# Four first-layer MLP products ahead of the last transposes, and first-layer staging moved to the other side of SBUF

## The chip, the cores and the metric

One Trainium2 chip, one of its cores. The metric is the device time of one execution in microseconds (us): the median of three runs of the kernel before is 3024.37 us (3020.51 to 3025.22). The engines are named as the profile names them: PE (TensorE; its weight loads are PEld), ACT (ScalarE), DVE (VectorE), POOL (GpSimd), and SP, the engine whose queue issues every DMA of this kernel, in order.

## The reference

One transformer layer on 2048 tokens of width 1024, all in float32. What matters here is its second half, after attention and pooling have been merged and projected:

```
x = layernorm(ALPHA * x + g1 * y, ln1_g, ln1_b)          # x1, the input of the MLP
u = layernorm(x) * (1 + scale) + shift                   # 2048 x 1024
h = square(relu(u @ w1)) @ w2                            # w1: 1024 x 4096, w2: 4096 x 1024
x = layernorm(ALPHA * x + g2 * h, ln2_g, ln2_b)
```

## The kernel before

**Numbers in two halves.** A float32 operand is split into a rounded high part (ACT casts it, line 59) and the rest (DVE subtracts, line 62). A product of two split operands is three matmuls: high by high, high by low, low by high.

**Seven products instead of eight.** Both MLP layers multiply 2 x 2 blocks with seven products (`ORDER = (1, 6, 2, 7, 5, 4, 3)`), which need sums of blocks. The sums of `u` ("combinations") are made by `u2_half` (line 922) and written to DRAM in `us_scr[c]`, one plane for each product. The sums of the weights `w1` are made in SBUF by `Pair.add` and `Pair.step` on POOL; the sums of `w2` by `w2_fill` (line 1173), which also stores two of them in DRAM (`t3_scr`, `t2_scr`) for later products.

**Stages.** The stage ahead of the MLP works on two token halves (`c` = 0, 1; 1024 tokens each). Its last loop projects (`out_mm`), then normalises one block of 128 tokens after another (`ln_affine` to x1, `ln1_u` to the normalised `xn`). `u2_half(h)` takes four blocks: for each of four pairs of channels `kp` it transposes on PE (line 929), scales on ACT into `u2f` (line 930), makes four sums on POOL into `u2s` (lines 935 to 938), and stores both (SP, lines 941 and 942). The second half of `c` = 0 waits in the list `late` and runs early in `c` = 1. The second half of `c` = 1 needs the last block, so `run(late)` stands at the end of the stage.

**First layer** (from `mp = ctx.enter_context(sbuf("mlp"))`). 32 pairs of weight column blocks: 16 on the first 1024 tokens, 16 on the second. `Pair.load` brings a pair's raw weights (`sraw`, 1 MB as two DMAs, line 1001), `step` splits one operand into a tile `R`, `prod` (line 1039) does 12 matmuls, and its sums and squares go into tiles of the tag `st`. `l_fill(c, p)` loads the combination of product `p` (`rw`, 1 MB, line 1085) and splits it into two tiles `La` or `Lb`. The list `seq` gives the order of the products: the first two pairs go together (p = 1 for both, p = 6 for both, and so on). Seven `R` steps and all seven `l_fill` stand ahead of the first product.

**Second layer.** For each `p`, eight products of 48 matmuls (`prod2`, line 1254). All eight use the eight weight tiles of `p` (`L2[p]`, from the same 11 `La` tiles); meanwhile `w2_fill` makes those of the next `p`, and `h_fill` loads and splits the stored first-layer results two products ahead. The first tiles of `p` = 1 are made during the last pair of the first layer (`w2_first`, line 1107; `h_first`).

**What sets the order.** PE's instructions follow the program from the first layer on (`manual_schedule`). Those of ACT, DVE, POOL and SP are ordered, when the kernel is built, by a planner that simulates times: an instruction can be put ahead of others that the program has earlier, as soon as its inputs and its tile are there. Tiles come from pools with a number of buffers for each tag. A pool whose space a closed pool held comes behind it in this order: the planner places the first instruction on its tiles after the last one on the closed pool's tiles. On the chip a new tile waits only for the old tiles at its own addresses. In the kernel before, the MLP's pools `mlp` and `mlp1` (left side of SBUF) come after all of `lp` (left), `ptp` and `rp` (right side) are closed, behind `run(late)`; `mlp2` comes after `mlp1` is closed (`m1.close()`).

Of the kernel before, what the change touches and what calls it, by code (L numbers as in the profile page):

```python
# [10 lines left out]
F32 = mybir.dt.float32  # L11
F32R = mybir.dt.float32r
# [4 lines left out]
P = 128  # L17
# [19 lines left out]
def block_kernel(  # L37
# [5 lines left out]
    pe, act, dve, pool, sp = nc.tensor, nc.scalar, nc.vector, nc.gpsimd, nc.sync  # L43
# [6 lines left out]
    us_scr = [tc.dram_tile([P, 7, 4, 512], F32, name=f"us_scr{c}") for c in range(2)]  # L50
    hs_scr = [[tc.dram_tile([P, 4, 16, P], F32, name=f"hs_scr{c}{p}") for p in range(7)] for c in range(2)]
    t2_scr, t3_scr = (tc.dram_tile([P, 16, 512], F32, name=n) for n in ("t2_scr", "t3_scr"))

    def sbuf(name, side="left"):
        return tc.tile_pool(name=name, bufs=1, side=side, reuse_waits="tile")

    def split(hi, lo, src, lo_eng=None, hi_eng=None):
        if hi_eng is None:
            act.copy(hi, src)  # L59
        else:  # L60
            hi_eng.tensor_copy(hi, src)
        (lo_eng or dve).tensor_tensor(lo, src, hi.bitcast(F32), ALU.subtract)  # L62
# [53 lines left out]
    def slot(where, i, shape, dt, name):  # L116
        pl, tag, n = where
        return pl.tile(shape, dt, name=name, tag=f"{tag}{i}", bufs=n)
# [214 lines left out]
    def run(units):  # L333
        for f in units:
            f()
# [277 lines left out]
    for n, (b, g) in enumerate(order):  # L613
# [4 lines left out]
        for tok in (PLAN[g] if b + 2 < NB else TPLAN).split():  # L618
            t, i = tok[0], int(tok[1:] or 0)
# [36 lines left out]
    lpx = ExitStack()  # L656
# [67 lines left out]
    late = []  # L724
    for c in range(2):
        t0 = c * CH
# [3 lines left out]
        xs, ys = ((rp, "a", 8), (lp, "b", 9)) if c == 0 else ((lp, "b", 9), (rp, "a", 8))  # L730
# [95 lines left out]
        for n in range(4):  # L826
            w = wcols(w_in, 2048 + n * 256)
            for jj in range(2):
                ps = [ps2("ps_ga") for _ in HALF]
                chan_mm(ps, w, jj * P, um)  # L830
                s = slot(ys, 0, [P, CH], F32, "sa")
# [8 lines left out]
        for kk in range(4):  # L840
            raw = raw_tile([P, 2, CH])
            sp.dma_start(raw, a_scr[:, 2 * kk:2 * kk + 2, t0:t0 + CH])
            for k in range(2):
                hv = []
                for h in range(2):
                    t = slot(xs, h, [P, 2, 512], F32R, "av")
# [4 lines left out]
        for n in range(4):  # L851
            w = wcols(w_ab, n * 256) if n else w_first
            for jj in range(2):
                j = 2 * n + jj
# [3 lines left out]
                for h, (a, m) in enumerate(HALF):  # L858
                    s = sa[j][:, a:a + m]
                    dve.tensor_tensor(s, ps[h], s, ALU.mult)  # L860
                    pool.tensor_tensor(s, s, m0[j][:, a:a + m], ALU.add)  # L861
                    t = slot(xs if c == 1 and j == 0 else ys, h, [P, 2, 512], F32R, "mg")
# [51 lines left out]
        xn = []  # L914
# [3 lines left out]
            normal(n, accs[b])  # L918
            xn.append(n)

        def u2_half(h, c=c, t0=t0, xn=xn, ys=ys):

            for kp in range(4):
                f = slot(ys, 0, [P, 2, 512], F32, "u2f")
                for kk in range(2):
                    k = 2 * kp + kk
                    ps = ps2("ps_u2", "u", 2)
                    for i in range(4):
                        pe.transpose(ps[:, i * P:(i + 1) * P], xn[4 * h + i][:, k * P:(k + 1) * P], ident)
                    act.activation(f[:, kk], ps, AF.Identity, scale=mod[:, 32 + k, 0:1], bias=mod[:, 24 + k, 0:1])  # L930
                v = f.rearrange("p k (b r t) -> p k b r t", r=2, t=P)
                a11, a12, a21, a22 = v[:, 0, :, 0], v[:, 1, :, 0], v[:, 0, :, 1], v[:, 1, :, 1]
                s = slot(ys, 1, [P, 4, 256], F32, "u2s")
                sv = [s[:, i].rearrange("p (b t) -> p b t", t=P) for i in range(4)]
                pool.tensor_tensor(sv[0], a21, a22, ALU.add)
                pool.tensor_tensor(sv[1], sv[0], a11, ALU.subtract)
                pool.tensor_tensor(sv[2], a11, a21, ALU.subtract)
                pool.tensor_tensor(sv[3], a12, sv[1], ALU.subtract)
                dst = us_scr[c][:, :, kp, h * 256:(h + 1) * 256]
                for pl, t in enumerate((a11, a12, a22)):  # L940
                    sp.dma_start(dst[:, pl].rearrange("p (b t) -> p b t", t=P), t)
                sp.dma_start(dst[:, 3:7], s)
# [5 lines left out]
        w2 = wcols(w_out, 512, gb[0][:, 512:768])  # L948
# [10 lines left out]
            if b == 5:  # L959
                u2_half(0)  # L960
        ln1_u(7)
        late = [lambda f=u2_half: f(1)]

    sp.dma_start(g2_scr, gb[1][0:1, :].rearrange("a d -> (a d)"))
    run(late)
    lpx.close()
    ptx.close()
    rpx.close()

# [5 lines left out]

    ORDER = (1, 6, 2, 7, 5, 4, 3)
    PLANE = {1: 0, 2: 1, 4: 2, 5: 3, 6: 4, 7: 5, 3: 6}
    mp = ctx.enter_context(sbuf("mlp"))
    m1 = ExitStack()
    m1p = m1.enter_context(sbuf("mlp1"))  # L980
    ms3 = ExitStack()
    ms3.enter_context(tc.manual_schedule(engines={mybir.EngineType.PE}))

    def rtile():
        return mp.tile([P, 2, 4, P], F32R, name="R", tag="R", bufs=8)

    def sttile(name):
        return m1p.tile([P, 512], F32, name=name, tag="st", bufs=14)

    w1v = w_mlp_in.rearrange("(k two p) n -> p two k n", two=2, p=P)  # L990

    class Pair:
# [3 lines left out]
            self.c, self.n, self.R = c, n, {}  # L996

        def load(self):
            self.raw = m1p.tile([P, 2, 4, 256], F32, name="sraw", tag="sraw", bufs=3)
            for k in range(2):  # L1000
                sp.dma_start(self.raw[:, k], w1v[:, k, :, self.n * 256:(self.n + 1) * 256])
            b11, b12, b21, b22 = self.b = [self.raw[:, k, :, h * P:(h + 1) * P] for k in range(2) for h in range(2)]
            self.op = {1: b11, 2: b21, 3: b22, 4: b11, 7: b12}

        def add(self):
            b11, b12, b21, b22 = self.b
            for p in (5, 6):
                self.op[p] = m1p.tile([P, 4, P], F32, name="ext", tag="ext", bufs=4)
            pool.tensor_tensor(self.op[5], b12, b11, ALU.subtract)
            pool.tensor_tensor(self.op[6], b22, self.op[5], ALU.subtract)  # L1010
            pool.tensor_tensor(b12, b22, b12, ALU.subtract)
# [69 lines left out]

    def l_fill(c, p):

        raw = m1p.tile([P, 4, 512], F32, name="rw", tag="rw", bufs=2)
        sp.dma_start(raw, us_scr[c][:, PLANE[p]])
        Lc[c][p] = []
        for j in range(2):
            if (p, j) in ((4, 1), (3, 0), (3, 1)):
                t = m1p.tile([P, 2, 2, 512], F32R, name="Lb", tag="Lb", bufs=3)
            else:  # L1090
                t = mp.tile([P, 2, 2, 512], F32R, name="La", tag="La", bufs=11)
            split(t[:, 0], t[:, 1], raw[:, 2 * j:2 * j + 2])
            Lc[c][p].append(t)


# [1 line left out]
    w2v = w_mlp_out.rearrange("(n two p) d -> p two n d", two=2, p=P)  # L1097
    L2 = {p: [] for p in ORDER}
    R2 = {}

    def latile():
        return mp.tile([P, 2, 2, 512], F32R, name="La", tag="La", bufs=11)

    def w2_first(j):

        raw = m1p.tile([P, 4, 512], F32, name="rw", tag="rw", bufs=2)
        sp.dma_start(raw, w2v[:, 0, 4 * j:4 * j + 4, 0:512])
        return [lambda z=z: w2_split(raw[:, 2 * z:2 * z + 2]) for z in range(2)]

    def w2_split(raw):  # L1110
        l = latile()
        split(l[:, 0], l[:, 1], raw)
        L2[1].append(l)

    def h_first(i):
        raw = m1p.tile([P, 16, P], F32, name="hr", tag="sraw", bufs=3)
        sp.dma_start(raw, hs_scr[0][PLANE[1]][:, i])
        R2[1, i] = []
        for k in range(0, 16, 4):
            t = rtile()  # L1120
            split(t[:, 0], t[:, 1], raw[:, k:k + 4])
            R2[1, i].append(t)
# [5 lines left out]
        q.load()  # L1128
    prep = [(p, q) for _, p, q in seq]
    AHEAD = 7  # L1130
    for i in range(AHEAD):
        if i % 2 == 0:
            l_fill(0, ORDER[i // 2])
        prep[i][1].step(prep[i][0])
    for p in ORDER[4:]:
        l_fill(0, p)
    for i, (g, p, q) in enumerate(seq):
        n = q.c * 16 + q.n
        if p == 1 and n + 2 < len(pairs):
            pairs[n + 2].load()  # L1140
        q.prod(p, Lc[q.c][p])
        if q is pairs[15]:
            l_fill(1, p)
        if i + AHEAD < len(prep):
            prep[i + AHEAD][1].step(prep[i + AHEAD][0])
        if q is pairs[31]:
            if p == 1:
                parts = w2_first(0) + w2_first(1)
            elif p == 6:
                run(parts[:2])  # L1150
                parts = parts[2:] + w2_first(2)
            elif p == 2:
                run(parts[:2])
                parts = parts[2:] + w2_first(3)
            elif p == 7:
                h_first(0)
                run(parts[:2])
            elif p == 5:
                run(parts[2:])
# [5 lines left out]
    NI = 8  # L1165

    def w2_tile(src):
        t = m2p.tile([P, 2, 512], F32, name="w2", tag="w2", bufs=4)
        sp.dma_start(t, src)
        return t  # L1170

# [28 lines left out]

    def h_fill(p, i):
        R2[p, i] = []
        for z in range(2):
            raw = m2p.tile([P, 8, P], F32, name="hraw", tag="hraw", bufs=3)
            sp.dma_start(raw, hs_scr[i // 4][PLANE[p]][:, i % 4, 8 * z:8 * z + 8, :])
            for k in (0, 4):
                t = rtile()
                split(t[:, 0], t[:, 1], raw[:, k:k + 4])
                R2[p, i].append(t)

    rows = []
    for name, v in (("g2", g2_scr), ("ln2g", ln2_g), ("ln2b", ln2_b)):
# [141 lines left out]
```

## Time and profile before

| | us |
|---|---|
| median of 3 runs | 3024.37 |
| the profiled execution | 3021.76 |
| its span, first to last instruction | 3020.0 |
| PE busy in the span | 2899.2 (96%) |
| DVE, POOL, ACT busy | 1817.9, 1382.5, 1365.8 |
| granted TensorE clock, mean over the span | 0.984 |

PE is the engine that is nearly always busy; the others have time to spare on the whole. The page's 40 slices show two places in the second half where PE's digit falls: slices 23 and 24 (7 and 6 tenths, about 1661 to 1812 us), where the stage ahead ends and the MLP begins. The granted clock is full nearly everywhere, and lower in slices where PE was idle. An idle stretch so costs twice: the wait, and the matmuls after it that run at half clock. An average over the span says nothing of a stage; the views below are all of short stretches.

### The profile page before, as it was taken

What the parts mean: (1) busy time and instruction counts of PE and PEld (TensorE: products, weight loads), DVE (VectorE), ACT (ScalarE), POOL (GpSimd) and SP (SyncE); (2) the same over time, 40 slices, a digit from 0 to 9 for tenths busy, and PEclk for the clock granted to TensorE, in tenths of its full rate; (3) what the DMA queues carried; (4) which work ended last, traced back from release to release, by engine and by line L of the source; (5) the groups of instructions that cost most, each with busy time, mean ns of one, the idle gap of its engine ahead of it and who ended that gap; (6) DMA issues with size and microseconds to landing.
All of it is one profiled execution on the core that took longest, in us unless ns stands there. A gap on an engine that the chain in (4) does not pass through costs nothing.

```text
span 3020.0 us, 42577 instructions
## 1 busy us (share of the span) xinstructions
PE 2899.2 (96%) x15336; PEld 2473.6 (82%) x15336; DVE 1817.9 (60%) x3201; ACT 1365.8 (45%) x2462; POOL 1382.5 (46%) x1638
## 2 busy tenths in 40 slices
PE   8899999999899999999999769999999989999998
PEld 5789989998888888888889758888888768888886
DVE  5578787877875444742144765558555453556675
ACT  4577777777751222332221455556555432233342
POOL 2867777777540014323033457666665340123244
PEclk9999999999999999999999889999999999999999
DMA  7111111112234433352132376547555684566663
GB/s 257 36 30 37 33 37 31 43 37 61 68 100 145 128 126 102 109 158 79 42 112 84 115 257 188 152 141 233 172 151 155 236 308 141 188 213 215 203 205 109
DMA packets 342663, 395.38 MB, mean 131 GB/s; under 512 B 16689, under 2 KB 276913, under 8 KB 340402
## 3 DMA queue, kind: packets, MB, share of 16 engines
q1 hardware_dynamic: 342450, 392.64, 40.8%
q8 instruction: 121, 1.98, 0.3%
q14 instruction: 92, 0.75, 0.1%
HBM read 275.13 MB, written 117.44 MB: 130 GB/s over the span
## 4 chain that ended last, share of the span: by engine, by line
PE 80%; DVE 7%; DMA 5%; POOL 3%; issue 3%; ACT 2%; SPq 0%; POOLq 0%; ACTq 0%; DVEq 0%
PE ps_h L1039 18%; PE ps_y L1254 16%; PE ps_o L503 4%; PE ps_pt L486 4%; PE ps_s L450 3%; PE ps_gp L688 2%; PE ps_ga L685 2%; PE ps_ga L688 2%; PE ps_ga L686 2%; PE ps_ab L685 2%; PE ps_ab L686 2%; PE ps_gp L685 2%; PE ps_ab L688 2%; PE ps_gp L686 2%; PE ps_s L451 2%
## 5 line engine op out<-in xcount | busy, mean ns | idle before, releaser
L1254 PE MATMUL ps_y<-La,R 128*128 128x512 f32 x2688 | 614.9, 391 | 15.5 <-ACT La L59 11.6
L1254 PEld LDWEIGHTS ps_y<-La,R 128*128 128x128 f32 x2688 | 506.5, 189 | 123.7 <-ACT La L59 12.8
L1039 PE MATMUL ps_h<-La,R 128*128 128x512 f32 x2112 | 488.4, 391 | 25.4 <-ACT La L59 22.1
L1039 PEld LDWEIGHTS ps_h<-La,R 128*128 128x128 f32 x2112 | 398.3, 189 | 110.3 <-ACT La L59 22.3
L62 DVE TENSOR_TENSOR R<-hraw,R 128x512 fp32r<-128x512 f32 x216 | 188.6, 883 | 153.9 <-ACT R L59 153.5
L62 DVE TENSOR_TENSOR pl<-ps_pt,ph 128x512 fp32r<-128x512 f32 x312 | 212.3, 685 | 70.6 <-ACT ph L59 68.6
L59 ACT CAST R<-hraw 128x512 fp32r<-128x512 f32 x216 | 131.9, 621 | 271.6 <-PE ps_y L1254 254.3
L465 POOL TENSOR_SCALAR s<-s,sm 128x640 f32<-128x640 f32 (+1 forms) x256 | 201.4, 796 | 102.1 <-DVE sm L464 53.8
L462 ACT ACTIVATE s<-s,sm 128x641 f32<-128x641 f32 (+1 forms) x256 | 209.9, 820 | 69.7 <-DVE sm L456 69.2
L861 POOL TENSOR_TENSOR sa<-sa,m 128x512 f32<-128x512 f32 x32 | 57.2, 1809 | 375.6 <-DVE sa L860 375.6
L456 DVE CUSTOM_DVE_ANT_0 s<-ps_s,mask,nsink 128x640 f32<-128x640 f32 (+1 forms) x256 | 211.3, 862 | 29.3 <-PE ps_s L451 29.0
L59 ACT CAST ph<-ps_pt 128x512 fp32r<-128x512 f32 x312 | 179.5, 580 | 108.5 <-PE ps_pt L486 105.3
L486 PE MATMUL ps_pt<-ident,s 128*128 128x128 f32 x1248 | 189.6, 274 | 12.2 <-DVE pl L62 7.8
L59 ACT CAST wh<-raw 128x2048 fp32r<-128x2048 f32 (+1 forms) x38 | 67.0, 1771 | 277.9 <-DMA raw<-w_in 75.7
L62 DVE TENSOR_TENSOR R<-sraw,R 128x512 fp32r<-128x512 f32 x160 | 147.0, 921 | 75.6 <-ACT R L59 75.2
L486 PEld LDWEIGHTS ps_pt<-ident,s 128*128 128x128 f32 x1248 | 151.3, 141 | 43.4 <-DVE pl L62 13.3
L62 DVE TENSOR_TENSOR wl<-raw,wh 128x2048 fp32r<-128x2048 f32 (+1 forms) x38 | 86.3, 2273 | 159.9 <-ACT wh L59 159.8
L59 ACT CAST R<-sraw 128x512 fp32r<-128x512 f32 x160 | 98.9, 621 | 153.1 <-PE ps_h L1039 95.2
L66 PE MATMUL ps_out<-wh,mg 128*128 128x256 f32 x512 | 143.1, 281 | 0.0
L67 PE MATMUL ps_out<-wl,mg 128*128 128x256 f32 x512 | 142.8, 280 | 0.0
L68 PE MATMUL ps_out<-wh,mg 128*128 128x256 f32 x512 | 142.6, 280 | 0.0
L1039 PE MATMUL ps_h<-Lb,R 128*128 128x512 f32 x576 | 136.1, 389 | 1.0 <-DVE cv L1057 1.0
(266 smaller groups left out, 7066.8 us busy)
## 6 DMA issues: line engine op xcount, KB each, us to landing
hraw<-hs_scr SPq DMA_DIRECT2D x108, 512.0 KB, 3.6
sraw<-w_mlp_in SPq DMA_DIRECT2D x64, 512.0 KB, 6.3
w<-w_mlp_out SPq DMA_DIRECT2D x64, 512.0 KB, 5.1
hs_scr<-s SPq DMA_DIRECT2D x96, 256.0 KB, 4.9
raw<-w_in SPq DMA_DIRECT2D x19, 1024.0 KB, 5.5
raw<-w_ada SPq DMA_DIRECT2D x16, 1024.0 KB, 5.2
rw<-us_scr SPq DMA_DIRECT2D x14, 1024.0 KB, 5.6
raw<-u_scr SPq DMA_DIRECT2D x8, 1032.0 KB, 5.9
```

What stands on the lines that cost most here:

```text
L59: act.copy(hi, src)
L62: (lo_eng or dve).tensor_tensor(lo, src, hi.bitcast(F32), ALU.subtract)
L66: pe.matmul(ps, sh, mh, start=first, stop=False)
L456: dve.tensor_tensor_reduce(out=s[:, 0:n], in0=pieces[z][2], in1=mk[z], op0=ALU.add, op1=ALU.min, scale=-1.0 / math.sqrt(HD), scalar=nsink[ ...
L462: act.activation(s[:, 0:n + 1], s[:, 0:n + 1], AF.Exp, bias=sm[:, 0, j:j + 1], scale=-1.0, accum_out=sm[:, 1, j:j + 1])
L465: pool.tensor_scalar(s[:, 0:n], s[:, 0:n], sm[:, 2, j:j + 1], 1.0, ALU.mult, ALU.mult)
L486: pe.transpose(pt[:, c:c + P], self.s.probs[2 * z + j][:, o:o + P], ident)
L685: pe.matmul(ps, wh[:, k, c:c + P], mh, start=k == 0, stop=False)
L686: pe.matmul(ps, wh[:, k, c:c + P], ml, start=False, stop=False)
L688: pe.matmul(ps, wl[:, k, c:c + P], mh, start=False, stop=k == KT - 1)
L1039: pe.matmul(ps, a, b, start=p in (1, 6, 5) and k == 0 and i == 0, stop=k == 3 and i == 2, skip_group_check=p not in (1, 6, 5))
L1254: pe.matmul(ps, a, b, start=n == 0 and z == 0, stop=n == 15 and z == 2)
```

## The change

`run(late)` moves from the end of the stage ahead into the loop over first-layer products, ahead of the fifth (`EARLY = 4`): p = 1 and p = 6 of the first two pairs stand ahead of the 32 transposes in PE's order. For `c` = 1, `u2_half(1)` writes its `u2f` and `u2s` into the left pool (`xs`) and not the right one, so that `rp` can be closed before it. On the right side, in the place of `rp`, two new pools take the weights' `sraw` (2 of 3 buffers), the tiles `R` (8), four `Le` tiles (the combinations of p = 1 and 6; later four of the 11 tiles for `w2`) and four of the 14 `st` tiles (`se`). The four raw halves of combinations 1 and 6 and the sums `ext` of the first two pairs use free buffers of `lp`. Only behind `run(late)` is `lp` closed and are `mlp` and `mlp1` opened; then come the other five `l_fill` and the loads of pairs 2 and 3. A combination is now loaded as two DMAs of 512 KB. The raw `w2` tiles use `rw` of `mlp` (4 buffers of 512 KB, as before in number) and the second layer's raw `h` uses the two 1 MB `sraw` buffers, one DMA where there were two: none of them is in `mlp2` any more.

```diff
@@ the stage ahead @@
-        def u2_half(h, c=c, t0=t0, xn=xn, ys=ys):
+        def u2_half(h, kps=range(4), c=c, t0=t0, xn=xn, ys=ys):
...
-            for kp in range(4):
+            for kp in kps:
...
-        late = [lambda f=u2_half: f(1)]
+        late = [lambda f=u2_half: f(1)] if c == 0 else [lambda kp=kp, f=u2_half, s=xs: f(1, (kp,), ys=s) for kp in range(4)]

     sp.dma_start(g2_scr, gb[1][0:1, :].rearrange("a d -> (a d)"))
-    run(late)
-    lpx.close()
     ptx.close()
     rpx.close()
@@ the first layer's pools @@
-    mp = ctx.enter_context(sbuf("mlp"))
+    ep = ctx.enter_context(sbuf("mlpr", side="right"))
+    def raw8(shape):
+        return ep.tile(shape, F32, name="sraw", tag="sraw", bufs=2)
+    def rwtile():
+        return mp.tile([P, 2, 512], F32, name="rw", tag="rw", bufs=4)
     m1 = ExitStack()
-    m1p = m1.enter_context(sbuf("mlp1"))
+    e1 = m1.enter_context(sbuf("mlpr1", side="right"))
...
-        return mp.tile([P, 2, 4, P], F32R, name="R", tag="R", bufs=8)
+        return ep.tile([P, 2, 4, P], F32R, name="R", tag="R", bufs=8)
+    m1p = None
+    sts = [0]
     def sttile(name):
-        return m1p.tile([P, 512], F32, name=name, tag="st", bufs=14)
+        n = sts[0] = (sts[0] + 1) % 14
+        pl, tag, bufs = (e1, "se", 4) if 1 <= n <= 4 else (m1p, "st", 10)
+        return pl.tile([P, 512], F32, name=name, tag=tag, bufs=bufs)
@@ Pair.load, Pair.add @@
-            self.raw = m1p.tile([P, 2, 4, 256], F32, name="sraw", tag="sraw", bufs=3)
+            shape = [P, 2, 4, 256]
+            self.raw = raw8(shape) if (16 * self.c + self.n) % 3 < 2 else m1p.tile(shape, F32, name="sraw", tag="sraw", bufs=1)
...
-            for p in (5, 6):
+            if m1p is None:
+                t = slot(xs, 1, [P, 2, 4, P], F32, "ext")
+                self.op.update({5: t[:, 0], 6: t[:, 1]})
+            for p in (5, 6) if m1p else ():
@@ l_fill @@
-        raw = m1p.tile([P, 4, 512], F32, name="rw", tag="rw", bufs=2)
-        sp.dma_start(raw, us_scr[c][:, PLANE[p]])
         Lc[c][p] = []
         for j in range(2):
-            if (p, j) in ((4, 1), (3, 0), (3, 1)):
+            half = slot(xs, 0, [P, 2, 512], F32, "rw") if m1p is None else rwtile()
+            sp.dma_start(half, us_scr[c][:, PLANE[p], 2 * j:2 * j + 2])
+            if p in (1, 6):
+                t = ep.tile([P, 2, 2, 512], F32R, name="Le", tag="Le", bufs=4)
+            elif (p, j) in ((4, 1), (3, 0), (3, 1)):
...
-                t = mp.tile([P, 2, 2, 512], F32R, name="La", tag="La", bufs=11)
+                t = mp.tile([P, 2, 2, 512], F32R, name="La", tag="La", bufs=7)
@@ w2_first, h_first: the same, two rwtile() and one raw8() @@
...
@@ the loop over the first layer's products @@
     AHEAD = 7
+    EARLY = 4
     for i in range(AHEAD):
-        if i % 2 == 0:
+        if i in (0, 2):
             l_fill(0, ORDER[i // 2])
         prep[i][1].step(prep[i][0])
-    for p in ORDER[4:]:
-        l_fill(0, p)
     for i, (g, p, q) in enumerate(seq):
         n = q.c * 16 + q.n
-        if p == 1 and n + 2 < len(pairs):
+        if i == EARLY:
+            run(late)
+            lpx.close()
+            mp = ctx.enter_context(sbuf("mlp"))
+            m1p = m1.enter_context(sbuf("mlp1"))
+            for z in ORDER[2:]:
+                l_fill(0, z)
+            for z in (2, 3):
+                pairs[z].load()
+        if i >= EARLY and n + 2 >= 4 and p == 1 and n + 2 < len(pairs):
             pairs[n + 2].load()
@@ the second layer @@
     def w2_tile(src):
-        t = m2p.tile([P, 2, 512], F32, name="w2", tag="w2", bufs=4)
+        t = rwtile()
...
     def h_fill(p, i):
         R2[p, i] = []
-        for z in range(2):
-            raw = m2p.tile([P, 8, P], F32, name="hraw", tag="hraw", bufs=3)
-            sp.dma_start(raw, hs_scr[i // 4][PLANE[p]][:, i % 4, 8 * z:8 * z + 8, :])
-            for k in (0, 4):
...
+        raw = raw8([P, 16, P])
+        sp.dma_start(raw, hs_scr[i // 4][PLANE[p]][:, i % 4])
+        for k in range(0, 16, 4):
...
```

## Rows read from the trace of the kernel before

**Rows 1.** Waits of PE over the span: line, waited for: us in total, times, longest.
```profile
PE ps_h L1039 <- ACT La L59: 22.1, 1, 22.1
PE ps_y L1254 <- ACT La L59: 11.6, 2, 6.8
```

**Rows 2.** Timeline of PE, 1700 to 1800: start us, us, engine, line, count [idle before].
```profile
1730.36 0.69 PE L929 MATMUL ps_u<-ident,xn 128*128 128x128 f32 x2 [2.89 <-ACT xn L900]
...
1759.25 0.79 PE L1039 MATMUL ps_h<-La,R 128*128 128x512 f32 x1 [22.06 <-ACT La L59]
1760.79 8.62 PE L1039 MATMUL ps_h<-La,R 128*128 128x512 f32 x24 [0.75 <-DVE La L62]
1771.53 23.21 PE L1039 MATMUL ps_h<-La,R 128*128 128x512 f32 x101 [2.13 <-DVE La L62]
```

**Rows 3.** Timeline of SP's queue, 1700 to 1800: start us, us, line, what, count.
```profile
1727.32 0.36 SPq L942 DMA_DIRECT2D us_scr<-u2s  x1
...
1740.12 3.09 SPq L942 DMA_DIRECT2D us_scr<-u2s  x3
1743.30 4.15 SPq L1001 DMA_DIRECT2D sraw<-w_mlp_in  x4
1747.49 1.68 SPq L1085 DMA_DIRECT2D rw<-us_scr  x2
```

**Rows 4.** Timeline of ACT, 1700 to 1800.
```profile
1750.67 0.62 ACT L59 CAST R<-sraw 128x512 fp32r<-128x512 f32 x1 [12.59 <-DMA sraw<-w_mlp_in]
...
1758.15 1.99 ACT L59 CAST La<-rw 128x1024 fp32r<-128x1024 f32 x2 [3.52 <-DMA rw<-us_scr]
```

**Rows 5.** Windows: PE, PEld, DVE, ACT, POOL busy (count), granted clock, DMA share, GB/s.
```profile
1740.00:1742.00 2.00, 0.00 (x0) 0.00 (x0) 0.00 (x0) 0.00 (x0) 2.00 (x4) 0.50 0.83 266
1764.00:1766.00 2.00, 2.00 (x6) 1.59 (x5) 2.00 (x2) 0.76 (x2) 1.92 (x3) 0.50 0.90 287
...
1776.00:1778.00 2.00, 2.00 (x10) 1.69 (x9) 1.28 (x3) 0.77 (x1) 0.00 (x0) 1.00 0.99 340
...
2500.00:2600.00 100.00, 100.00 (x443) 82.78 (x442) 43.39 (x59) 30.18 (x45) 3.45 (x2) 1.00 0.50 163
```

**Rows 6.** Timeline of PE, 2355 to 2500.
```profile
2377.60 21.92 PE L1254 MATMUL ps_y<-La,R 128*128 128x512 f32 x96
2400.82 0.73 PE L1254 MATMUL ps_y<-La,R 128*128 128x512 f32 x2 [1.30 <-ACT R L59]
2403.16 73.30 PE L1254 MATMUL ps_y<-La,R 128*128 128x512 f32 x322 [1.61 <-DVE R L62]
2481.27 0.79 PE L1254 MATMUL ps_y<-La,R 128*128 128x512 f32 x1 [4.80 <-ACT La L59]
...
2493.09 7.10 PE L1254 MATMUL ps_y<-La,R 128*128 128x512 f32 x21 [0.46 <-DVE La L62]
```

**Rows 7.** Timeline of SP's queue, 2355 to 2500.
```profile
2385.12 0.51 SPq L1027 DMA_DIRECT2D hs_scr<-s  x1
...
2387.38 2.57 SPq L1169 DMA_DIRECT2D w<-w_mlp_out  x3
```

**Rows 8.** Timeline of ACT, 2355 to 2500.
```profile
2373.23 2.00 ACT L59 CAST La<-rw 128x1024 fp32r<-128x1024 f32 x2 [0.68 <-DMA rw<-w_mlp_out]
...
2458.88 1.05 ACT L59 CAST La<-w 128x1024 fp32r<-128x1024 f32 x1 [0.31 <-PE ps_y L1254]
```

**Rows 9.** Timeline of POOL, 2355 to 2500.
```profile
2400.20 2.36 POOL L1182 TENSOR_TENSOR w<-w,w 128x1024 f32<-128x1024 f32 x1
...
2488.37 2.34 POOL L1182 TENSOR_TENSOR w<-w,w 128x1024 f32<-128x1024 f32 x1 [0.43 <-DMA w<-w_mlp_out]
```

**Rows 10.** The page, DMA issues: count, KB each, median us from issue to landing.
```profile
hraw<-hs_scr SPq DMA_DIRECT2D x108, 512.0 KB, 3.6
sraw<-w_mlp_in SPq DMA_DIRECT2D x64, 512.0 KB, 6.3
...
rw<-us_scr SPq DMA_DIRECT2D x14, 1024.0 KB, 5.6
```

More of the change, by code (lines that the diff above doesn't have):

```diff
@@ L1082, in l_fill @@
     def l_fill(c, p):
-        raw = m1p.tile([P, 4, 512], F32, name="rw", tag="rw", bufs=2)
-        sp.dma_start(raw, us_scr[c][:, PLANE[p]])
         Lc[c][p] = []
         for j in range(2):
-            if (p, j) in ((4, 1), (3, 0), (3, 1)):
+            half = slot(xs, 0, [P, 2, 512], F32, "rw") if m1p is None else rwtile()
[3 more added lines that the diff above has]
+            elif (p, j) in ((4, 1), (3, 0), (3, 1)):
                 t = m1p.tile([P, 2, 2, 512], F32R, name="Lb", tag="Lb", bufs=3)
             else:
-                t = mp.tile([P, 2, 2, 512], F32R, name="La", tag="La", bufs=11)
-            split(t[:, 0], t[:, 1], raw[:, 2 * j:2 * j + 2])
+                t = mp.tile([P, 2, 2, 512], F32R, name="La", tag="La", bufs=7)
+            split(t[:, 0], t[:, 1], half)
             Lc[c][p].append(t)
@@ L1099, in block_kernel @@
     R2 = {}
+    lns = [0]
     def latile():
-        return mp.tile([P, 2, 2, 512], F32R, name="La", tag="La", bufs=11)
+        n = lns[0] = (lns[0] + 1) % 11
+        pl, tag, bufs = (ep, "Le", 4) if 1 <= n <= 4 else (mp, "La", 7)
+        return pl.tile([P, 2, 2, 512], F32R, name="La", tag=tag, bufs=bufs)
     def w2_first(j):
-        raw = m1p.tile([P, 4, 512], F32, name="rw", tag="rw", bufs=2)
-        sp.dma_start(raw, w2v[:, 0, 4 * j:4 * j + 4, 0:512])
-        return [lambda z=z: w2_split(raw[:, 2 * z:2 * z + 2]) for z in range(2)]
+        raws = [rwtile() for _ in range(2)]
+        for z in range(2):
+            sp.dma_start(raws[z], w2v[:, 0, 4 * j + 2 * z:4 * j + 2 * z + 2, 0:512])
+        return [lambda t=t: w2_split(t) for t in raws]
     def w2_split(raw):
@@ L1115, in h_first @@
     def h_first(i):
-        raw = m1p.tile([P, 16, P], F32, name="hr", tag="sraw", bufs=3)
+        raw = raw8([P, 16, P])
         sp.dma_start(raw, hs_scr[0][PLANE[1]][:, i])
@@ L1202, in h_fill @@
         R2[p, i] = []
-        for z in range(2):
-            raw = m2p.tile([P, 8, P], F32, name="hraw", tag="hraw", bufs=3)
-            sp.dma_start(raw, hs_scr[i // 4][PLANE[p]][:, i % 4, 8 * z:8 * z + 8, :])
-            for k in (0, 4):
-                t = rtile()
-                split(t[:, 0], t[:, 1], raw[:, k:k + 4])
-                R2[p, i].append(t)
+        raw = raw8([P, 16, P])
+        sp.dma_start(raw, hs_scr[i // 4][PLANE[p]][:, i % 4])
+        for k in range(0, 16, 4):
+            t = rtile()
+            split(t[:, 0], t[:, 1], raw[:, k:k + 4])
+            R2[p, i].append(t)
     rows = []
```

## The prediction

> **What bounds the kernel now.** PE is busy for 96% of the span, so time is lost only where PE waits, or runs at half clock behind a wait. I read first the waits of PE over the span: the longest single one is 22.1 us ahead of the first layer's first product, the next group 11.6 us in two waits of the second layer, both for a split of a weight or combination tile [rows 1]. Then the timelines of the two stretches, engine by engine, to see what those splits had waited for, and the windows for the clock.
>
> *First place, the end of the stage ahead.* After the last block is normalised PE transposes from 1730.36, and then has nothing until 1759.25 [rows 2]. SP's queue says why: the last sums of `u2_half(1)` are stored until 1743.21, and only then come the weights' `sraw` (1743.30), which nothing in the kernel writes, and combination 1 (1747.49) [rows 3]. The weights reach ACT at 1750.67, the combination at 1758.15 [rows 4]. The wait is one of queue order and of DMA, not of data: those inputs were ready long before. [...] The first four products end 23 matmuls into the row at 1771.53, and 23.21 us for 101 matmuls is 0.2298 us each: 1776.8 [rows 2].
>
> *Second place, the start of the second layer.* 448 matmuls (96 + 2 + 322 + 1 + 5 + 1 + 21 in that timeline) take from 2377.60 to 2500.19, 122.6 us [rows 6]. At the rate of the next window, 443 in 100 us [rows 5], they would take 101.1. So 21.5 us are lost: 11.6 in the two waits for `La` [rows 1], the rest in small waits and at half clock. The `La` tiles of p = 6 come late: their first raw loads leave at 2387.38, behind the last store of `mlp1` at 2385.12 [rows 7]. Each of the eight fills needs three loads, two POOL passes and two stores through four buffers; their second passes start from 2400.20 to 2488.37, 12.6 us apart [rows 9]. The last ends at 2490.7, but p = 6 had asked for its tiles from 2468 on (the 286 matmuls of p = 1 left at 2403.16, at 73.3 us for 322 [rows 6]).
>
> **The change, first place.** The products put ahead fill no idle PE before 1735: they get their weights too late. The step by step:
> - *The weights' issue.* The right pools can open once the last tile of `rp` has been used: the store of the first half's last sums, 1727.32 + 0.36 [rows 3]. So `sraw` leaves at 1727.7 and not at 1743.3. The raw combinations 1 and 6 go to free buffers of `lp`, which come free earlier; I cost them at nothing, hidden behind the normalising of the last blocks. If that cover is gone they queue behind `sraw`, 4.2 us more by the distance of the two in the old queue (1747.49 - 1743.30).
> - *Landing and split.* `sraw` lands in 6.3 us in the median [rows 10]; in the old queue the first cast came 7.4 us after the first issue [rows 3, 4], behind 1.5 MB of stores. I take 6.3 and 0.7 for the cast (0.62 [rows 4]) and the wake-up: first product at 1734.7. Bounds: 3.6 us (`hraw`, the quickest of that size) and 7.4 plus the 4.2 above.
> - *Four products.* Before, 17.5 us (1759.25 to 1776.8), of it 0.75 + 2.13 of waits for splits [rows 2]: 14.7 without. The clock is at its lower level here as it was there. I take 14.7, since the combinations are split ahead: end at 1749.4. Bounds: 11.0 (48 at full rate) and 17.5.
> - *Transposes, sums and stores, now behind the products.* From the first transpose after the last block to the end of the last store it took 12.85 us (1730.36 to 1743.21) [rows 2, 3]. The 32 transposes, 8 evictions, 16 sums and 16 stores are the same, so the last store is out at 1762.3. Bound above: 15.3, if four `R` splits beside them hold POOL up for as long as their casts take (0.62 each); below I leave 12.85, as POOL's sums are one behind the other.
> - *The second fence.* `mlp` and `mlp1` open only behind that store. What is queued behind it: the loads of combinations 2, 7, 5, 4, 3 and of pairs 2 and 3, and behind these PE's fifth product. A half of 512 KB lands in between 3.6 us (`hraw`) and 6.3 (`sraw`) [rows 10]; the old load took 10.6 from 1747.49 with 2 MB ahead [rows 3, 4], which is the upper end. I take 5.2 as 1.5 MB of stores are in flight; then the cast, 1.05: fifth product at 1768.6. In the 19 us from the fourth product to there PE has 32 transposes and nothing else: a new hole, most of it idle, where the old one was 22 us.
> - *The clock.* It fell within such a hole before, so the fifth product starts at half clock. Before, 25 matmuls from 1759.25 took 12.28 us with 2.88 of waits, 9.4 against 5.75 at the full rate [rows 2]: 3.65 lost, and paid a second time here. The fifth product is worth 1772.3.
> - *Sum:* 1776.8 - 1772.3 = 4.5 us gained. With all lower ends 1732.0 + 11.0 + 12.85 + 3.6 + 1.05 + 3.65 = 1764.2, a gain of 12.6; with all upper ends 1740.0 + 17.5 + 15.3 + 10.6 + 1.05 + 3.65 = 1788.1, a loss of 11.3.
>
> **Second place.** The raw `w2` tiles and raw `h` are no longer in `mlp2`, so their loads need not wait for its opening. `w2_first` frees its raw buffers with the casts from 2373.23 on [rows 8] and SP stands idle there; I put the first loads of p = 6 at 2374, 13 us earlier. The chain of eight fills moves by as much until the 11 weight tiles are full: fills 3, 4 and 5 then hold finished sums in `rw` until p = 1 begins its last product and frees tiles (in the old trace the cast at 2458.88). Before, fill 5's passes came only after that; now they are done. From there two fills of about 9 us with their loads, half overlapped, end near 2477, when p = 6 asks for its last tile (2468 + 14 x 3 x 0.2298 = 2478). The waits for `hraw` at 2400 to 2403 go too (1.30 + 1.61 [rows 6]), as the 1 MB of `h` can be loaded during the last pair. I leave 3 us of the 21.5: 18.5 gained. Bounds: 21.5; and below zero, a loss of 2, if the four buffers set the pace after 2458.88 as before and one 1 MB piece of `h` (5.6 us against 3.6 [rows 10]) stands ahead of a `w2` load.
>
> **Elsewhere** the tiles keep their numbers (3 `sraw`, 14 `st`, 11 `La`, 8 `R`) and are taken in the same turn, and PE is busy without a gap in windows like 2500 to 2600 [rows 5]: nothing, within 2 us. Sum against the profiled execution: 3021.8 - 4.5 - 18.5 = 2998.8. The median of the runs shown is 2.6 above that execution; I say 3000.
>
> [...] Five combinations of 1 MB become ten pieces. In the trace pieces in flight together move 340 GB/s [rows 5], so 7.3 MB (with two pairs) take 21.6 us, against 31.3 for the ten products until pair 2 (27.6 and 3.65 of clock). [...] The windows speak against pieces going one by one.
>
> **The rivals.**
> - *The four buffers still set the second place's pace.* For it: before, the fills came 12.6 us apart [rows 9] against 11 for a product. Against: five of the eight need only be done by 2458. Then only the `h` wait goes, 2.9: 3021.8 - 4.5 - 2.9 = 3014.
> - *Both holes nearly close:* 3021.8 - 12.6 - 21.5 = 2988. Against it: the lower ends would have to meet.
> - *The loads behind the second fence don't keep up.* One by one at 5.6 us for 1 MB [rows 10], 7 MB take 39.2 us against 31.3: 8 us, 3008. For it: four buffers only, and pairs 2 and 3 in the same queue. Against: the 340 GB/s.
> - *Slower: the fences hold for everything.* If the planner places nothing on the moved tiles before the closed stages' last instruction, the weights leave as late as before (1743.3), the first product starts at 1751 and transposes, sums, stores and five combinations all stand behind four products: 1751 + 14.7 + 12.85 + 5.2 + 1.05 + 3.65 = 1788.5, 11.7 late, and the second place gains nothing: 3033. It decides at the first place from a first product later than 1739 on. For it: in both old queues the first load on new tiles stood right behind the last store on the old ones [rows 3, 7]. Against: the moved tiles' pools close earlier or not at all.
>
> **How the numbers follow.** The forecast 0.45, with a range of its own of 2992 to 3008; the four buffers 0.20; both holes close 0.10; loads don't keep up 0.10; fences 0.15. About 0.2% (6 us) is what a measurement of this kernel tells from no change: 3018 to 3030. Faster: 0.45 + 0.14 of the second case + 0.10 + 0.09 = 0.78. Same: 0.06 of the second, 0.05 of the last (its second place partly gained), 0.01 = 0.12. Slower: 0.10 of the last. The range 2987 to 3020 takes in all but the fences and the far tails.
>
> **What would show it.** First `sraw` issue at 1727 to 1729; first product 1732 to 1738, all four before any transpose of the last half; a PE hole of over 8 us ahead of the fifth product, whose release is an `La` of combination 2 behind an SP row that follows the last `us_scr` store at once. In the second layer, first `w2` load of p = 6 near 2374 less the shift, and less than 4 us of PE waits for `La` up to the second product of p = 6. Wrong would be: a first product after 1740, a fifth after 1777, or p = 6 waits of over 8 us.

## The result, and the profile after

The changed kernel takes 3042.09 us (median of six runs, 3040.11 to 3046.33), the kernel before in the same runs 3024.80; the ratio is 1.0059, 95% interval [1.0049, 1.0069]. It is slower by some 17 us, where 3000 and a gain were forecast. The span of the profiled execution is 3041.1 us, the mean granted clock 0.984 as before.

The first place came out nearly as forecast. PE's timeline (start us, us, engine, line, count, wait ahead):

```profile
1737.17 1.22 PE L1054 MATMUL ps_h<-Le,R 128*128 128x512 f32 x2 [19.26 <-ACT R L59]
1738.66 12.05 PE L1054 MATMUL ps_h<-Le,R 128*128 128x512 f32 x46 [0.28 <-DVE R L62]
1750.55 1.03 PE L929 MATMUL ps_u<-ident,xn 128*128 128x128 f32 x8
...
1771.71 0.80 PE L1054 MATMUL ps_h<-La,R 128*128 128x512 f32 x1 [15.18 <-ACT La L59]
...
1809.71 11.62 PE L1054 MATMUL ps_h<-La,R 128*128 128x512 f32 x42 [2.02 <-ACT cx L1059]
```

and SP's queue in the same stretch:

```profile
1728.76 4.08 SPq L1013 DMA_DIRECT2D sraw<-w_mlp_in  x4
1752.12 4.76 SPq L941 DMA_DIRECT2D us_scr<-u2f  x9
...
1761.40 3.08 SPq L942 DMA_DIRECT2D us_scr<-u2s  x3
1764.58 3.16 SPq L1102 DMA_DIRECT2D rw<-us_scr  x4
```

The weights leave at 1728.76 and not at 1743.30 [rows 3], the first product starts 22 us earlier than in [rows 2], and then PE stands 15.18 us ahead of product 5. In the second layer the two short `R` waits of [rows 6] are gone, and one wait for `La` of 7.84 us is left:

```profile
2392.98 98.71 PE L1283 MATMUL ps_y<-La,R 128*128 128x512 f32 x426
2499.54 0.80 PE L1283 MATMUL ps_y<-La,R 128*128 128x512 f32 x1 [7.84 <-ACT La L59]
2500.80 19.38 PE L1283 MATMUL ps_y<-La,R 128*128 128x512 f32 x72 [0.47 <-DVE La L62]
```

So PE waits less than before (its idle time in the span is 115.1 us, 120.8 before), yet the time is longer. The page's first section has PE busy for longer with the same number of instructions (2899.2 before):

```profile
PE 2926.0 (96%) x15336; PEld 2473.6 (81%) x15336; DVE 1809.5 (60%) x3201; ACT 1367.6 (45%) x2462; POOL 1385.4 (46%) x1638
```

Windows without a wait show where. Their columns are us, PE busy (count), granted clock, DMA share, GB/s; first the kernel before, then the changed one:

```profile
1900.00:2000.00 100.00, 100.00 (x443) 1.00 0.54 160
2600.00:2700.00 100.00, 100.00 (x443) 1.00 0.61 202
```

```profile
1900.00:2000.00 100.00, 100.00 (x432) 1.00 0.51 148
2600.00:2700.00 100.00, 100.00 (x432) 1.00 0.56 196
```

PE is busy for 100% at full clock in both, and does 432 matmuls where it did 443. That is a loss which no list of waits shows. The groups by operand, 1900 to 2350, say which matmuls are slower (mean ns of one in the last figure ahead of the idle time); first the kernel before, then the changed one:

```profile
L1039 PE MATMUL ps_h<-La,R 128*128 128x512 f32 x1570 | 360.1, 389 | 0.3 <-ACT cx L1044 0.3
L1039 PE MATMUL ps_h<-Lb,R 128*128 128x512 f32 x414 | 97.6, 389 | 0.0
```

```profile
L1054 PE MATMUL ps_h<-La,R 128*128 128x512 f32 x966 | 229.7, 396 | 1.2 <-ACT cx L1059 1.2
L1054 PE MATMUL ps_h<-Le,R 128*128 128x512 f32 x552 | 129.3, 390 | 0.0
L1054 PE MATMUL ps_h<-Lb,R 128*128 128x512 f32 x416 | 100.9, 395 | 0.0
```

From one start to the next it is 226.7 ns on average for every operand before; in the changed kernel 233 to 234 for La and Lb, 228 to 229 for tiles in the four Le buffers. The built programs give the addresses. Before, La, Lb and R differ by a multiple of 512 bytes. After, R stands on the right side with Le, a multiple of 512 from it; La and Lb on the left differ from R by 96 bytes more than a multiple of 512. Matched by the start of the n-th MLP matmul, the profiled execution of the changed kernel against that of the one before stands so (us, positive is later); e5 is the changed kernel with that difference made a multiple of 512, e9 the best version (both below):

| start of MLP matmul | changed | e5 | e9 |
|---|---|---|---|
| 126 (early in the first layer) | -2.3 | -2.9 | -12.0 |
| 2687 (end of the first layer) | +15.4 | +4.8 | -4.7 |
| 3300 (behind the second place) | +8.9 | -4.4 | -19.3 |
| 5375 (last) | +21.4 | -2.5 | -19.3 |

### The profile page after: what moved, and what is told of

It is laid out like the page before. It is cut to its first block, busy times and chain, and to the rows that moved or that the text cites. A ratio compares the mean times of both kernels' runs of the same rounds, so it can differ in the third digit from the quotient of the medians.

```text
span 3041.1 us, 42469 instructions
## 1 busy us (share of the span) xinstructions
PE 2926.0 (96%) x15336; PEld 2473.6 (81%) x15336; DVE 1809.5 (60%) x3201; ACT 1367.6 (45%) x2462; POOL 1385.4 (46%) x1638
## 4 chain that ended last, share of the span: by engine, by line
PE 79%; DVE 7%; DMA 6%; POOL 4%; issue 2%; ACT 1%; SPq 0%; POOLq 0%; DVEq 0%; ACTq 0%
PE ps_h L1054 18%; PE ps_y L1283 15%; PE ps_o L503 4%; PE ps_pt L486 4%; PE ps_s L450 3%; PE ps_gp L688 2%; PE ps_ga L685 2%; PE ps_ga L688 2%; PE ps_ga L686 2%; PE ps_ab L685 2%; PE ps_ab L686 2%; PE ps_gp L685 2%; PE ps_ab L688 2%; PE ps_gp L686 2%; PE ps_s L451 2%
## 5 line engine op out<-in xcount | busy, mean ns | idle before, releaser
L1283 PE MATMUL ps_y<-La,R 128*128 128x512 f32 x2688 | 627.0, 395 | 9.3 <-ACT La L59 7.8
L62 DVE TENSOR_TENSOR R<-sraw,R 128x512 fp32r<-128x512 f32 x384 | 334.9, 877 | 221.6 <-ACT R L59 220.2
L59 ACT CAST R<-sraw 128x512 fp32r<-128x512 f32 x384 | 237.2, 620 | 451.4 <-PE ps_y L1283 306.8
L1054 PE MATMUL ps_h<-La,R 128*128 128x512 f32 x1344 | 323.3, 398 | 19.0 <-ACT La L59 15.2
L1054 PEld LDWEIGHTS ps_h<-La,R 128*128 128x128 f32 x1344 | 254.2, 189 | 82.6 <-ACT La L59 15.4
L1054 PE MATMUL ps_h<-Le,R 128*128 128x512 f32 x768 | 182.1, 393 | 19.5 <-ACT R L59 19.3
L1054 PEld LDWEIGHTS ps_h<-Le,R 128*128 128x128 f32 x768 | 145.2, 189 | 52.3 <-ACT R L59 19.7
L486 PEld LDWEIGHTS ps_pt<-ident,s 128*128 128x128 f32 x1248 | 151.2, 141 | 44.5 <-DVE pl L62 14.2
```

Source lines behind the costliest of these rows:

```text
L486: pe.transpose(pt[:, c:c + P], self.s.probs[2 * z + j][:, o:o + P], ident)
L1054: pe.matmul(ps, a, b, start=p in (1, 6, 5) and k == 0 and i == 0, stop=k == 3 and i == 2, skip_group_check=p not in (1, 6, 5))
L1283: pe.matmul(ps, a, b, start=n == 0 and z == 0, stop=n == 15 and z == 2)
```

## The experiments

Ratios are against the kernel before, timed on the same chip beside each, with 95% intervals.

**The place of the operands.** Seven kernels move tiles by some bytes; nothing is added but one small memset.

*e1, 32 bytes at the top of the right pool.*
```diff
+    pool.memset(ep.tile([P, 8], F32, name="pad"), 0.0)   # changed kernel, behind the AHEAD loop
```


> The changed kernel with one 32-byte tile allocated last at the top of the right-hand pool, so that R, Le and sraw stand 32 bytes lower and both matmul operands begin at multiples of 64 bytes, as before the change; instructions, order and distances between the operands stay. Theory A (a matmul is slower when its moving operand, La or Lb, and its weights, R, differ by 32 bytes modulo 64): the 3600 matmuls of that kind go from 232 to 226.7 ns, at clock 1.00 the stretch 1900 to 2000 holds 443 first-layer matmuls and not 432, and the time is about 3042 - 24 = 3018 (3014 to 3022). Rival B (R lies on the other side, or farther from La, or another region is slower): 432 per 100 us stay, time 3042. Rival C (other engines' or DMAs' traffic at that time): 3042 too.

3040.14 us, 1.0051 [1.0037, 1.0065]: theory A missed. La and Lb stay where they were, so their difference from R is now 128 modulo 512, where it was 96, and they are as slow as without the pad:
```profile
L1054 PE MATMUL ps_h<-La,R 128*128 128x512 f32 x966 | 229.6, 395 | 2.4 <-DVE cu L1062 1.6 <-ACT cx L1059 0.8
L1054 PE MATMUL ps_h<-Le,R 128*128 128x512 f32 x552 | 128.8, 389 | 0.0
L1054 PE MATMUL ps_h<-Lb,R 128*128 128x512 f32 x414 | 100.4, 395 | 0.0
```
The start at a multiple of 64 is not what counts. That Le keeps its rate beside a slow La spoke for the relation of the two operands, at a longer period.

*e2, e3, e7, e4: the kernel before, with 32, 64 or 256 bytes between La and R, or 32 ahead of both.*
```diff
+            pool.memset(mp.tile([P, 8], F32, name="pad"), 0.0)   # e2; 16 in e3, 64 in e7; e4: ahead of La
```


> The kernel before with a 32-byte tile between La and R in their pool: R, and with it Lb, begin 32 bytes past a multiple of 64, La doesn't. Nothing else is changed. Theory A: the 4800 matmuls that read La take some 232 ns instead of 226.7, the 576 that read Lb (moved along with R) stay at 226.7; 4800 x 5.5 to 6 ns = 26 to 29 us, time 3051 to 3054. Rivals B and C (side, distance, traffic): 3025, unchanged.

3053.03, 1.0091 [1.0078, 1.0105]. The kernel before is made 28 us slower by 32 bytes; Lb, moved along with R, keeps its rate within the same stretch:
```profile
L1039 PE MATMUL ps_h<-La,R 128*128 128x512 f32 x1518 | 358.0, 396 | 0.0
L1039 PE MATMUL ps_h<-Lb,R 128*128 128x512 f32 x422 | 100.1, 390 | 0.0
```
Rivals B and C are out: side, distance and traffic are those of the kernel before.

> The kernel before with 64 bytes in the same place. Theory A, if what counts is the difference modulo 64: 226.7 ns throughout, 3025. If it is modulo 128 or more: slow as with 32 bytes, 3050 or more. Rivals B and C: 3025.

3052.48, 1.0091 [1.0077, 1.0105]: the period is not 64.

> The kernel before with the 32 bytes ahead of La, so that La, Lb and R all begin 32 bytes past a multiple of 64. Theory A (only the difference of the two operands counts): 226.7 to 228 ns, 3025 to 3031. Rival D (each operand has to begin at a multiple of 64 by itself): all 5376 matmuls slow, 3055 or more. Rivals B and C: 3025.

3025.39, 1.0001 [0.9992, 1.0010]: moved by 32 bytes together they cost nothing, so it is not the start of one operand by itself.

> The kernel before with 256 bytes between La and R: the difference is 256 modulo 512 for the 4800 matmuls that read La and 0 for the 576 on Lb. If the period is 256 bytes: 226.7 ns throughout, 3025. If it is 512: 233 ns on La, 3052 to 3054.

3024.84, 1.0004 [0.9995, 1.0013], 443 matmuls in each of the windows 1900 to 2000, 2200 to 2300 and 2600 to 2700: 256 is as good as 0.

*e5 and e12: the changed kernel with a difference of 0 modulo 256, by moving the right pool (416 bytes) or the left one (160).*

> The changed kernel with a tile of 416 bytes allocated last at the top of the right-hand pool: R, Le and sraw stand 416 bytes lower, so that La, Lb and Le all differ from R by a multiple of 512 bytes, as La and Lb did in the kernel before. The runs so far showed 226.7 to 228 ns a matmul where the difference was a multiple of 512 (whatever the place of R), 233 to 234 ns at 32, 64, 96 and 128 bytes more or less. Theory A2 (the difference modulo 512 or 256 decides): all 5376 matmuls near 226.7 ns; 3600 x 7 + 1744 x 1.4 ns = 27.6 us less than the changed kernel, time 3014 (3011 to 3018). Rival B (the side or the distance): 3040.

3018.27, 0.9980 [0.9971, 0.9989]; 443 again:
```profile
1900.00:2000.00 100.00, 100.00 (x443) 1.00 0.53 156
2600.00:2700.00 100.00, 100.00 (x443) 1.00 0.57 200
```


> The changed kernel with 160 bytes at the bottom of its left pool, so that La and Lb stand 160 bytes higher and R, Le and sraw stay where the change put them. La then differs from R by a multiple of 256 bytes. Theory A3 (the difference modulo 256 decides, whichever operand moves): all matmuls near 226.7 ns, 3018 as e5. Rival (the place of R, or what e5 moved besides): 3040.

3019.78, 0.9985 [0.9976, 0.9994]. Whichever operand is moved, the 22 to 24 us come back. What holds the 18 us that e5 still lacks to the forecast is the question of the next four.

**The first place.** *e6: as e5, `EARLY = 0`, the transposes ahead of all products.*

> As e5, and with no product ahead of the last transposes (EARLY 0 in place of 4): the transposes, the last stores and the closing of the pools come straight after the stage ahead, the four products on Le follow, and the loads for product 5 run beside them. Theory: product 5 then starts about 1755 and not 1771.7, the 15 us wait goes, 3014 - 16 = 2998 (2994 to 3004); putting the four products ahead of the transposes cost more than it gave. Rival: the loads behind the last stores wait for something else of the stage ahead, product 5 stays after 1765 and the time at 3008 or more.

3018.79, 0.9983 [0.9974, 0.9992]: missed; the rival came true. Product 5 starts at 1769.09. The transposes end 13 us earlier than in e5, but the last store is out only 2.6 us earlier (1761.51, in e5 1764.15): POOL, with the weights' sums between its 16 `u2s`, works until 1760.8. Two lines of its timeline there, and the last:
```profile
1743.30 0.73 POOL L937 TENSOR_TENSOR u2s<-u2f 128x256 f32<-128x256 f32 x1
...
1747.64 1.19 POOL L936 TENSOR_TENSOR u2s<-u2s,u2f 128x256 f32<-128x256 f32 x1
...
1758.76 2.08 POOL L938 TENSOR_TENSOR u2s<-u2f,u2s 128x256 f32<-128x256 f32 x3
```

*e8: as e6, a fifth staging buffer in the second layer.*
```diff
-        t = rwtile()
+        w2n[0] += 1
+        t = m2p.tile([P, 2, 512], F32, name="w2", tag="w2", bufs=1) if w2n[0] % 5 == 0 else rwtile()
-        return m2p.tile([P, 512], F32, name=name, tag="C", bufs=24)
+        return m2p.tile([P, 512], F32, name=name, tag="C", bufs=23)
```


> As e6, with a fifth staging buffer for the second layer's weights (every fifth load; one output tile fewer, 23 of 24). Theory F (the four shared buffers hold the fills of product 6 back): of the wait for La at 2499 of the changed kernel (7.8 us) and the low clock behind it, half to all goes, 3 to 9 us less than e6. Rival G (the transfers themselves: DMA share 1.01 and 0.98 from 2400 to 2440): the wait stays within 2 us, and so does the time.

3010.99, 0.9960 [0.9947, 0.9974], 8 us less than e6 by the medians (5.3 by the last matmul of the profiles). Theory F held. PE's waits for tiles of the second layer, e6 and then e8 (in all, times, longest):
```profile
PE ps_y L1284 <- ACT La L59: 7.7, 1, 7.7
```
```profile
PE ps_y L1286 <- ACT La L59: 2.7, 1, 2.7
```

*e9 and e10: as e8, the 16 `u2s` on DVE, with `EARLY` 0 and 4.*
```diff
-                pool.tensor_tensor(sv[0], a21, a22, ALU.add)
+                eng = dve if c and h else pool
+                eng.tensor_tensor(sv[0], a21, a22, ALU.add)   # and so the other three
```


> As e8 (no product ahead of the transposes, aligned, fifth buffer), with the 16 combinations u2s behind the last transposes on DVE and not on POOL. In the run without it POOL worked without a pause from 1734 to 1761 on u2s, ext and sraw, the last u2s ended at 1760.8 and the loads for product 5 followed. Theory P (POOL holds the last stores back, and these the loads): the last store goes out by 1750 to 1753, product 5 starts at 1758 to 1762 and not 1770.9, 8 to 12 us less, 2999 to 3003. Rival H (the wait is the trip of stores and loads through memory, whatever engine adds): within 2 us of e8, 3011.

3003.53, 0.9935 [0.9921, 0.9948]: 7.5 us less than e8, the fastest version, 21 us under the kernel before. Product 5 starts at 1762.31 and not at 1770.86 as in e8, with 5.42 us to wait, and SP's loads leave behind the last store at 1756.64, 6.2 us sooner than in e8 (1762.81):
```profile
1745.37 11.52 PE L1055 MATMUL ps_h<-Le,R 128*128 128x512 f32 x48
1762.31 0.80 PE L1055 MATMUL ps_h<-La,R 128*128 128x512 f32 x1 [5.42 <-ACT La L59]
```
```profile
1756.19 0.36 SPq L943 DMA_DIRECT2D us_scr<-u2s  x1
1756.64 2.17 SPq L1103 DMA_DIRECT2D rw<-us_scr  x4
```
The last store was put at 1750 to 1753; it came at 1756 as DVE had the splits of R to do between (0.68 us each, and 1.75 while POOL worked). Theory P held in kind; the gain is just under the 8 to 12 us that it gave.

> The same with the four products ahead of the transposes, as in the changed kernel (EARLY 4). There the transposes end at 1756.5 and their copies on ACT at 1757, so DVE can end the last u2s at about 1758 and not 1761: product 5 at 1768 to 1769, 2 to 3 us less than with POOL, 3008. So by theory P the four early products cost 5 to 9 us beside e9; by rival H the two orders come out within 2 us of each other.

3011.64, 0.9956 [0.9944, 0.9969]: 8 us behind e9. With the products first, DVE ends its last `u2s` at 1762.2, not 1758, and then the store stands behind three `u2f` stores in SP's queue:
```profile
1763.03 2.35 SPq L942 DMA_DIRECT2D us_scr<-u2f  x3
1765.48 0.45 SPq L943 DMA_DIRECT2D us_scr<-u2s  x1
1766.02 2.69 SPq L1103 DMA_DIRECT2D rw<-us_scr  x4
```
Product 5 starts at 1772.75. From the first transpose behind the products to product 5 that is 20.8 us (from 1751.91), and 21.0 in e5 (1750.23 to 1771.25), where POOL adds: in this order moving the sums gains nothing. The order that gives the change its name costs 8 us when DVE adds; when POOL adds (e5, e6) it costs nothing that can be measured.

*e11: the kernel before with those sums on DVE, the same edit.*

> The kernel before, with the 16 last u2s on DVE and nothing else. There POOL's 16 u2s end at 1742.8 and the last store is out at 1743.2; on DVE (0.41 us each in the run before this one, where POOL was idle) they can end behind ACT's last copy, some 3 to 4 us earlier, and all that follows moves by as much. Theory: 3 to 4 us of the gain of e9 (21 us against the kernel before) need nothing of the change, time 3020 to 3022; the other 17 come from the moved pools and the fills of the second layer. Rival: the order of the queues behind it eats them, 3024; or DVE alone gives most of it, 3012 or less.

3023.82, 0.9994 [0.9985, 1.0004]: nothing that can be measured; its last store is out at 1741.55, 1.7 us earlier: DVE's last `u2s` ends at 1738.55, but SP's queue issues the 12 `u2f` and 4 `u2s` stores one behind the other, from 1730.86 until then. So the gain of e9 is not that of DVE alone. The kernel before with a fifth buffer for `w2` was not run: how much of the 8 us of e8 it would have had without the change stays open.

## Why the prediction was wrong

**The step that failed** is "Elsewhere the tiles keep their numbers (3 `sraw`, 14 `st`, 11 `La`, 8 `R`) and are taken in the same turn, and PE is busy without a gap in windows like 2500 to 2600 [rows 5]: nothing, within 2 us." It was put at 0 and cost 33.6 us between the profiled executions (23.9 + 7.7 + 2.0 below); the two places gave 12.1 back (2.9 + 9.2), which leaves, but for rounding, the 21.4 us by which the last matmul is late. The medians are only 17.3 apart: the profiled execution of the kernel before is 3.0 under its median, that of the changed one 1.0 above. The three terms:

- *The rate of 3600 of 5376 matmuls:* +23.9 us (+21.4 for the changed kernel less -2.5 for e5; 23.8 by their medians). Being busy without a gap says nothing of the rate (PE is busy for 100% in both kernels' windows); the number of matmuls in the window does (443 and 432). The prediction used the 443 of [rows 5] as a constant, though the change moved one operand of every MLP matmul. Shown by e2, e5, e7 and e12 from both kernels and both operands.
- *Waits in the first layer:* +7.7 (e5, from -2.9 to +4.8). "In the same turn" was wrong: with 14 buffers split into 4 and 10, the third pair's `cx` falls on the buffer of the first pair's `cx`, where before it fell on another's. ACT waits for a store, in e5 as in the changed kernel:
```profile
ACT cx L1059 <- DMA hs_scr<-cx: 3.6, 1, 3.6
```
PE waits 2 us for ACT (the last row of the first fence), and the clock falls to 0.60 for 1810 to 1814. By the starts of the matmuls this place costs 4.4 us in e5, and a like wait near 2084 the other 3.3. The traces show these; no run took them away by itself.
- *A late wait for `La`* between matmuls 4400 and 4800: +2.0; it is gone in e8, so it hung on the four buffers.

**First place:** right in kind. Forecast against measured: weights' issue 1727.7 and 1728.76, first product 1734.7 and 1737.17, last store out 1762.3 and 1764.48, product 5 1768.6 and 1771.71, gain 4.5 and 2.3 to 2.9. The hole and the second fall of the clock were there (0.50 for 1736 to 1740, 1.00 for 1748 to 1752, 0.50 again for 1760 to 1764 with PE idle), and the stretch from the first of these transposes to the end of the last store, put at 12.85 us, took 13.93 (1750.55 to 1764.48). What it did not price is the other order. Here POOL is done with the weights' sums ahead of that stretch, waits for the first `u2f`, and then does its 16 `u2s` without a pause:
```profile
1752.17 0.73 POOL L937 TENSOR_TENSOR u2s<-u2f 128x256 f32<-128x256 f32 x1 [3.58 <-ACT u2f L930]
...
1762.69 1.41 POOL L938 TENSOR_TENSOR u2s<-u2f,u2s 128x256 f32<-128x256 f32 x2
```
With the sums on DVE the same stretch takes 14.0 us (e10). With the transposes first, POOL has the weights' sums to do between them (e6), and taking the `u2s` off POOL moves the fence (e9).

**Second place:** 18.5 us forecast, 9.2 came (e5, +4.8 to -4.4). The first load of p = 6 left 7 us ahead of the layer (2385.91), sooner than said. But the last of the eight second passes starts 103.1 us into the layer (2496.07 - 2392.98), against 110.8 before [rows 6, 9], and ends at 105.4; the prediction had the fills end about 99 us into it (2477 - 2377.6). POOL's waits in that stretch, 2390 to 2500, name the loads:
```profile
POOL rw L1210 <- DMA rw<-w_mlp_out: 33.6, 7, 10.2
POOL rw L1212 <- DMA rw<-w_mlp_out: 15.2, 4, 5.9
```
This is the rival of the four buffers, about half true: the fifth buffer brings the gain of this place from 10.3 us (e6, by the starts of the same two matmuls) to 14.2 (e8). What holds the rest of the 18.5 was not tried.

**The other rivals.** The fences held nothing back at the first place. The loads behind the second fence kept up: behind product 5 no product of the first layer waits for an `La` but once, 0.47 us, and the pieces of 512 KB, four of them issued within 3.16 us and landing in 5.6 us in the median, moved 404 GB/s there. The window:
```profile
1772.00:1774.00 2.00, 1.53 (x4) 0.84 (x4) 1.50 (x2) 1.40 (x2) 0.00 (x0) 0.50 1.00 404
```
The chance of slower, 0.10, hung on that one rival of the fences; the real cause was in no case.

## What to carry to other kernels

When a change moves operands, compare the count of matmuls per 100 us in windows without a wait before looking at waits, and keep the distance of moving operand and weights at the one that was fast: here 32 bytes cost the kernel before 28 us, and a dummy tile gave the changed one 22 to 24 back. Before moving work past a fence, ask what the last work ahead of it hangs on: the four products filled a hole of PE, but the sums and stores behind them took 14 us whichever engine added, and moving the sums to DVE paid only with the transposes first. A ring of buffers cut in two is not the same ring.

## What the runs showed of the hardware

- In the MLP of this kernel (512 columns, clock 1.00 in the windows), a matmul takes 226.7 ns from one start to the next where moving tile and weights differ by a multiple of 256 bytes of SBUF address (0 and 256 tried: 443 matmuls in each window of 100 us), and 233 to 234 ns, 3% more, at 32, 64, 96 and 128 (modulo 512; 32 and 64 in the other direction; 430 to 434 in the same windows, most of which hold tiles with a difference of 0 too). Such tiles beside slow ones, `Le` in the changed kernel, take 228 to 229.
- Why the difference counts, and how far this holds, is open. All `R` tiles have one remainder, so the runs cannot tell a matmul's own weights from those that PEld loads beside it (PEld is busy for 82.78 of PE's 100 us in [rows 5]). In the stage ahead (lines 685 to 688, 512 columns too) the trace of the kernel before has 228 to 235 ns by difference, and 231 at 0 and 256. There the moving tiles themselves stand 4160 bytes apart; it wasn't tried.
- While POOL and DVE both work, each took longer for the same sum: a `u2s` of 128x256 takes 0.73 us on POOL where DVE has nothing to do (1743.30 in e6) and 1.19 beside DVE's splits (1747.64, the fence of e6); on DVE it takes 0.41 with POOL idle, and 1.49 beside POOL. The 1.19 us are less than the two alone one after the other (0.73 and, for such a split, 0.68). No run shows why. Two lines of e9:
```profile
1736.53 1.49 DVE L936 TENSOR_TENSOR u2s<-u2f 128x256 f32<-128x256 f32 x1
...
1748.99 0.41 DVE L938 TENSOR_TENSOR u2s<-u2f 128x256 f32<-128x256 f32 x1
```
